# One-core hybrid encoder layer: per-layer embedding transposed first, exponentials split between ACT and DVE, query and key transposes on other PSUM banks, a new slab order

## The chip, the core and the metric

One core of a Trainium2 chip runs the whole layer. The time is the device time of one execution in microseconds (us); three executions of the kernel before gave 777.26, 777.6 and 778.51. Engines: PE (TensorE, matmuls and transposes), ACT (ScalarE), DVE (VectorE), POOL (GpSimd), SP (SyncE, which issues the DMAs).

## The reference, cut to what matters

One layer on 512 tokens of width 1024, all float32:

- h = RMSNorm(x); one projection of h gives attention q (8 heads), k, v (2 heads each) and gate az, delta-rule q, k, v (dq, dk, dv, 8 heads of 128) with decay and beta, gate dz, and two merge gates gA and gB.
- Branch A: q and k are normalised per head, rotated, softmax attention, times SiLU(az), projected (yatt).
- Branch B: short convolution of 5 taps and SiLU on dq, dk, dv, L2 norm, a gated delta rule in chunks, run forward and backward and summed, norm, times SiLU(dz), projected (ydn).
- Merge: sigmoid(gA) * A + sigmoid(gB) * B, projection (out), norm, added to x.
- Per-layer embedding: x + RMSNorm(sigmoid(x W_pg) * (p W_pp)). Here p is 512 x 256; the kernel calls p W_pp "ple" and x W_pg "pg".

## The kernel before, in words

Every large matrix product is done in three passes in a split format: each operand is cut into a high part (ACT casts it to fp32r) and a low part (DVE or POOL subtracts the high part), and PE adds low*high, high*low and high*high. A weight slab is 128 output columns: 512 KB come by DMA into one of two `wraw` buffers, `loader` (L416) and `split` (L211) make `whi` (ACT) and `wlo` (POOL or DVE), two buffers each, and `gemm_t` (L452) runs 24 matmuls of 512 columns into one of five PSUM banks called `mm`. Three further banks are called `aux`.

The order of all instructions is made ahead of time by a small planner, `Flow` (L35). Each part of the work is a generator with a priority (a lower number goes first); the planner keeps a calendar per engine from costs written in the code, and issues the part of the best priority that is ready. The engines then run their instructions in that order, each waiting for its operands on semaphores. `W` reserves DVE and POOL together, `Q` is a DMA issue on SP. Priorities stand in `PR` (L147), and `stream` (L1783) runs, at priority 10, the list `ORDER` (L138): 56 slabs (dk, dq, dv are convolutions; az, dz, gA, gB are gates), the blocks kv, q0, q1, then ydn, yatt, out, pg.

Around the stream, in time:

- Start: `warm_up` (L1708) runs transposes of the identity until planner time WARM. `h_part` (L330) broadcasts the norm's weight over the partitions with two matmuls of one row (L341), `x_norm` (L380) squares x on ACT and scales it on DVE with that broadcast, h is transposed (L357). `ple_part` (L1166) transposes p (L1176) and runs its eight products (L1191 to L1193) at priority 11, below the stream.
- `decay` (L589), and `prep` (L817): the decay factors E of the delta rule, 16 chunks of 128 x 512. A chunk is loaded, masked on POOL, and `exps` (L837) takes eight ACT instructions of 128 x 64, since each half of each head has its own bias `cj`.
- `conv_tail` (L723): per convolution slab, on ACT and DVE, with a transpose.
- The delta rule for head group 0, then 1: `phase_a` (L868), with a substitution of 30 steps on DVE, and `phase_b`; then `phase_y` (L1128).
- `kv_tail` (L1268) and `q_tail` (L1311): norm and rotation of a block that lies in an `mm` bank, then a transpose into another `mm` bank, and the split from there.
- `att_head` (L1367), eight heads, beside the ydn slabs.
- The end: `pg_job` (L1682), whose last tile goes in two halves through `pg_last` (L1650).

Of the kernel before, what the change touches and what calls it, by code (L numbers as in the profile page):

```python
# [16 lines left out]
NT = 4  # L17
# [118 lines left out]


ORDER = """  # L138
dq0 dq3 gB0 dq1 dk1 dq2 dk0 dk2 dk3 dv2 dz4 dk4 dk7 dz3 dv3 dv0
gA5 dz7 dk6 gA3 gB4 az6 dz2 az5 gA2 dv1 dq5 dq4 gA1 dk5 dq6 dq7  # L140
dz0 az2 gA7 dz1 az0 dv7 gB1 dv4 vec az1 az3 dz5 gA0 kv dv5 gB7
dv6 gA4 gB5 az4 gB6 gB3 q0 dz6 gA6 q1 az7 gB2 free_h ydn6 ydn4 ydn7
ydn0 ydn2 ydn5 ydn3 ydn1 yatt0 yatt3 yatt4 yatt1 yatt2 yatt7 yatt6 yatt5 out0 out1 pg0
pg1
"""
OUT0 = 'ydn7 ydn3 ydn3 yatt3'
PR = dict(dec=7, dm1=11, y=4, conv=6, gate=0, kv=9, q=6, head=0, ple=11, prep=4, tab=7)  # L147
GAP = 0.0
X_DVE = ()
WARM = 8.4  # L150
W1 = 0
COOL, HOT = 1.5, -3


@with_exitstack
def layer(ctx, tc, x, p, wt, wba, wn, wpp, npre, rows, qkn, hd16, npost, pnorm, dnorm, cs, out):
# [17 lines left out]
    def G(dur, dep, fn, *a, **k):  # L174
        return op("POOL", dur, dep, fn, *a, **k)

    def Q(kb, dep, o, i):

        t = op("DGE", 0.46, dep, sync.dma_start, o, i)
        return op("DMA", kb * 0.3, t + 0.5, None) + 1.3  # L180

    sb = ctx.enter_context(tc.tile_pool(name="sb", bufs=1))
# [142 lines left out]
        load["dnn"] = Q(0.1, 0.0, dnn, dnorm.rearrange("(p o) -> p o", o=1))  # L325
        first.set(F.now)

    first = Event()

    def h_part():  # L330
        yield "ev", first
        for i in range(4):
            yield "get", f"u{i}"
            (hTh, hTl)[i // 2].append(unit(i, [128, 4, 512], F32R))
        npr, tn = load["npr"]
        yield "at", tn + 0.2
        nb = []
        for half in range(2):
            yield "get", "mm"
            nb.append(bank("mm"))  # L340
            pe.matmul(nb[half], ones[0:1, :], npr[0:1, half * 512:half * 512 + 512], start=True, stop=True)  # L341
        yield "pe", 1.8
        free("blk")
        tn = F.now
        sc = {}
        sc_ev = [Event() for _ in range(NT)]
        spawn(x_norm(sc, sc_ev, nb, tn), 0)
        for t in range(NT):
            xt = load["x", t][0]
            yield "ev", sc_ev[t]  # L350
            for half in range(2):
                yield "at", sc[t, half] + 0.3
                yield "get", "aux"
                pt = bank("aux", [128, 4, 128])
                for j in range(4):
                    k = half * 4 + j
                    pe.transpose(pt[:, j, :], xt[:, k * 128:(k + 1) * 128], ident)  # L357
                yield "pe", 0.45
                cc = slice(t * 128, (t + 1) * 128)
                _, te = split(pt, hTh[half][:, :, cc], hTl[half][:, :, cc], F.now, 512)  # L360
                free("aux", te)
                if t == NT // 2 - 1:
                    h2_ev[half].set(te + 0.2)
                if t == NT - 1:
                    h_ev[half].set(te + 0.2)
        for tag in ("u4", "u5"):
            free(tag)
        rw, t = load["rw"]
        yield "at", t
        yield "get", "aux"  # L370
        pt = bank("aux", [128, 128])
        pe.transpose(pt, rw, ident)
        free("f2", F.now + 0.4)
        yield "pe", 0.11
        t = A(0.2, 0.0, act.copy, cw, pt)
        free("aux", t)
        G(0.1, load["dnn"], pool.tensor_scalar, out=dnn, in0=dnn, scalar1=0.5, scalar2=None, op0=ALU.mult)
        return t
# [434 lines left out]
    LTs, tE = {}, {}  # L813
# [3 lines left out]
    def prep(g, d):  # L817


        away = (g, d) == (1, 1)  # L820
        yield "ev", dec_ev
        if g == 1:
            yield "ev", E_ev[0, 1]
            if d == 0:
                yield "ev", spilled
        u = 16 if away else LTu[g, d]
        yield "get", f"u{u}"
        lt = unit(u, [128, 16, 128])
        sgn = 1 if d == 0 else -1
        for c in range(NT):  # L830
            E = lt[:, 4 * c:4 * c + 4, :]
            t = Q(2, late["CI"], E, CI[d, c, 4 * g:4 * g + 4].unsqueeze(0).to_broadcast([128, 4, 128]))
            yield "at", t - 1.0
            t = G(0.66, t, pool.affine_select, out=E, in_=E, compare_op=ALU.is_ge, fill=-1e30, base=0,
                  pattern=[[0, 4], [sgn, 128]], channel_multiplier=-sgn)

            def exps(E=E, c=c):  # L837
                for h in range(4):
                    for i in range(2):
                        e = E[:, h, i * 64:i * 64 + 64]  # L840
                        act.activation(e, e, AF.Exp, bias=cj[:, d, c, 4 * g + h, i:i + 1])  # L841

            t = A(1.64, t, exps)
            if away:
                t = Q(2, t, E1[c], E)
            tE[g, d, c] = t
        if away:
            free("u16", t)
            spilled.set(F.now)
            yield "get", f"u{LTu[g, d]}"  # L850
            lt = unit(LTu[g, d], [128, 16, 128])
            for c in range(NT):
                tE[g, d, c] = Q(2, tE[g, d, c], lt[:, 4 * c:4 * c + 4, :], E1[c])
        LTs[g, d] = lt
        yield "ev", nj_ev[g]
        for c in range(NT):
            E = lt[:, 4 * c:4 * c + 4, :]

            def scaled(E=E, c=c):
                for h in range(4):  # L860
                    act.activation(E[:, h, :], E[:, h, :], AF.Copy, scale=Nj[:, g, d, c, h:h + 1])

            tE[g, d, c] = either(tE[g, d, c], ("POOL", 1.05, pool.tensor_mul, E, E, bc(Nj[:, g, d, c])), ("ACT", 1.1, scaled))
        E_ev[g, d].set(F.now)

    spilled = Event()

    def phase_a(g):  # L868
        yield "ev", E_ev[g, 0]
# [50 lines left out]
            dve.tensor_sub(w[:, 0:m, m + 1:], w[:, 0:m, m + 1:], tt[:, 0:m, 0:31 - m])  # L920

        chains[0] += 1
        for m in range(30, 0, -1):
            t = W(0.32 + 2 * m * (31 - m) * 0.00104, t - 0.1, step, m)
            yield "at", t - 1.0
# [202 lines left out]
    def phase_y(g, be):  # L1128
# [9 lines left out]
        for c in range(NT):  # L1138
            def scaled(c=c):
                for h in range(4):  # L1140
                    act.activation(o[:, c, h], o[:, c, h], AF.Copy, scale=f[:, c, h:h + 1])

            t = A(1.15, t, scaled)
        us = ((4, 5), (7, 8))[g]
        for u in us:
            yield "get", f"u{u}"
# [16 lines left out]
        y_ev[g].set(t + 0.2)  # L1163


    def ple_part():  # L1166
        yield "ev", first
        yield "get", "u16"
        pT = ple["pT"] = unit(16, [128, 2, 2, 512], F32R)
        pr = ple["p"]  # L1170
        for t_ in range(NT):
            yield "at", ple["tp"] + 0.2
            yield "get", "mm"
            pt = bank("mm", [128, 2, 128])
            for j in range(2):
                pe.transpose(pt[:, j, :], pr[:, t_, j * 128:(j + 1) * 128], ident)  # L1176
            yield "pe", 0.25
            cc = slice(t_ * 128, (t_ + 1) * 128)
            _, t = split(pt, pT[:, 0, :, cc], pT[:, 1, :, cc], F.now, 256)
            free("mm", t)  # L1180
        free("u15")
        yield "at", t + 0.3
        for half in range(2):
            yield "ev", slab["ple", half][0]
            hi, lo = slab["ple", half][1]
# [82 lines left out]
    def kv_tail(t, o, tev):  # L1268
# [15 lines left out]
        free("mm", te)  # L1284
        te = W(0.35, max(te, ts), dve.tensor_mul, kr, kr, sak[:, t, :].unsqueeze(2).to_broadcast([128, 2, 128]))
        yield "at", te + 0.3
        yield "get", "mm"
        pt = bank("mm", [128, 2, 128])
        for h in range(2):
            pe.transpose(pt[:, h, :], kr[:, h, :], ident)  # L1290
        free("f2", F.now + 0.3)
        yield "pe", 0.22
        cc = slice(t * 128, (t + 1) * 128)
        _, te = split(pt, akT[:, 0, :, cc], akT[:, 1, :, cc], F.now, 256)
        free("mm", te)
        return te + 0.2

    att_ev = {}
# [12 lines left out]
    def q_tail(b, t, o):  # L1311
# [8 lines left out]
        te = yield from rope(qs, tabs[0], t, 4, qr, tq)  # L1320
        free("mm", te)
        yield "at", te + 0.3
        yield "get", "mm"
        pt = bank("mm", [128, 4, 128])
        for h in range(4):
            pe.transpose(pt[:, h, :], qr[:, h, :], ident)
        free("f2", F.now + 0.5)
        yield "pe", 0.436
        cc = slice(t * 128, (t + 1) * 128)
        _, te = split(pt, qh[:, :, cc], ql[:, :, cc], F.now, 512)  # L1330
        free("mm", te)
        return max(te, ts) + 0.2


# [315 lines left out]
    def pg_last(t, half, ob, ev):  # L1650
# [25 lines left out]
        for z, at, f in ((late["ob"], 512, V), (ob, 768, V), (z0[:, 0:256], 0, W), (z0[:, 256:512], 256, W)):  # L1676
            x_ = xa[:, at:at + 256]
            tr = f(0.4, tr, dve.scalar_tensor_tensor, out=x_, in0=z, scalar=rs, in1=x_, op0=ALU.mult, op1=ALU.add)
            Q(1, tr, out[t * 128:(t + 1) * 128, at:at + 256], x_)
        return tr  # L1680

    def pg_job(half, us):  # L1682
        if half == 0:
            yield "get", "u4"
            late["z0"] = unit(4, [128, 4, 512])
        for t in range(NT):
            yield "ev", att_ev["x1", t]
            if half == 0 or t < NT - 1:
                o = yield from gemm_n(f"pg{half}", t, sel(x1Th), sel(x1Tl))
                spawn(pg_tail(half, t, o, late["pno_ev"]), 5)  # L1690
        if half == 1:
            t, ev = NT - 1, None
            yield "get", "go"
            e = late["e"] = tile("go", [128, 512])
            late["te"] = Q(2, 0.0, e, eD[t, :, 512:1024])
            yield "get", "c2"
            late["sq"] = tile("c2", [128, 512])
            for i in range(2):
                o = yield from gemm_n("pg1", t, sel(x1Th), sel(x1Tl), cols=slice(i * 256, i * 256 + 256))
                ev = spawn(pg_last(t, i, o, ev), 5)  # L1700
# [31 lines left out]
    spawn(second(), 1)  # L1732
    spawn(phase_y(0, ch0), PR["y"])
    spawn(phase_y(1, y1), PR["y"])
    spawn(ple_part(), PR["ple"])
    for g in range(2):
        for d in ((0, 1), (1, 0))[g]:
# [103 lines left out]
```

## Time and profile before

| what | us |
|---|---|
| median of three runs | 777.6 |
| profiled execution, its own time | 777.5 |
| its span, first to last instruction | 775.7 |
| PE busy | 756.2 |
| DVE busy | 462.5 |
| ACT busy | 360.0 |
| POOL busy | 302.3 |

The span is what the instructions fill; 1.8 us lie around it. An engine counts as busy while an instruction of it is in flight; PE at half clock is busy too, so the granted clock is read beside it.

### The profile page before, as it was taken

The numbers are of one execution on the slowest core, as the hardware profiler recorded it, in microseconds if no ns is written. First come the engines' busy times: TensorE is split into PE (matmuls) and PEld (weight loads), VectorE is DVE, ScalarE is ACT, GpSimd is POOL, SyncE is SP. The second block draws the span as 40 slices with busy tenths as digits, with TensorE's granted clock in tenths as the row PEclk, the third lists the DMA queues.
The fourth block names the chain that finished last, engine by engine and source line by source line (L and its number), as shares of the span: only waits on it lengthen the run. The fifth ranks groups of instructions, "written<-read, shape, count | busy, mean of one in ns | idle before, by whom it ended". The sixth has DMA issues, their size and how long they took to land.

```text
span 775.7 us, 11989 instructions
## 1 busy us (share of the span) xinstructions
PE 756.2 (97%) x4543; PEld 631.2 (81%) x4543; DVE 462.5 (60%) x902; ACT 360.0 (46%) x719; POOL 302.3 (39%) x274
## 2 busy tenths in 40 slices
PE   8998999999999999999999999999999999999995
PEld 6786888888789888888788887778888888888885
DVE  5535767896866677795984543627766734313434
ACT  6477467633552554332542235335556632332422
POOL 4343567302311463102521155557345645561511
PEclk9999999999999999999999999999999999999998
DMA  7272246745310244556220234424233366553213
GB/s 268 96 217 98 81 157 204 200 166 170 104 50 23 78 149 110 187 153 175 86 95 14 68 109 130 127 96 163 82 110 122 110 209 212 198 160 131 95 46 130
DMA packets 53898, 100.50 MB, mean 130 GB/s; under 512 B 21009, under 2 KB 21969, under 8 KB 53842
## 3 DMA queue, kind: packets, MB, share of 16 engines
q1 hardware_dynamic: 53842, 99.75, 39.9%
q8 instruction: 35, 0.57, 0.3%
q14 instruction: 21, 0.17, 0.1%
HBM read 80.83 MB, written 18.91 MB: 129 GB/s over the span
## 4 chain that ended last, share of the span: by engine, by line
PE 80%; ACT 7%; DVE 6%; DMA 2%; issue 2%; POOL 2%; SPq 0%; POOLq 0%; DVEq 0%; ACTq 0%
PE mm L476 14%; PE mm L478 14%; PE mm L477 14%; PE mm L496 4%; PE mm L498 4%; PE mm L497 4%; DVE f L101 3%; ACT u L841 2%; PE mm L515 2%; PE mm L516 2%; PE mm L514 2%; PE aux L1062 2%; PE mm L1415 2%; PE aux L1094 2%; PE aux L1080 1%
## 5 line engine op out<-in xcount | busy, mean ns | idle before, releaser
L101 POOL TENSOR_TENSOR wlo<-wraw,whi 128x1024 fp32r<-128x1024 f32 x68 | 162.6, 2392 | 288.2 <-ACT whi L101 275.8
L476 PE MATMUL mm<-u,wlo 128*128 128x512 f32 x576 | 233.4, 405 | 6.1 <-POOL wlo L101 3.0
L478 PE MATMUL mm<-u,whi 128*128 128x512 f32 x576 | 225.8, 392 | 0.0
L477 PE MATMUL mm<-u,whi 128*128 128x512 f32 x576 | 225.3, 391 | 0.0
L101 ACT CAST whi<-wraw 128x1024 fp32r<-128x1024 f32 x84 | 88.0, 1050 | 126.9 <-PE mm L478 72.0
L476 PEld LDWEIGHTS mm<-u,wlo 128*128 128x128 f32 x576 | 108.7, 189 | 27.1 <-POOL wlo L101 4.2
L478 PEld LDWEIGHTS mm<-u,whi 128*128 128x128 f32 x576 | 108.5, 188 | 23.6
L477 PEld LDWEIGHTS mm<-u,whi 128*128 128x128 f32 x576 | 108.9, 189 | 20.0
L101 DVE SCALAR_TENSOR_TENSOR f<-mm,cw,f 128x510 f32<-128x510 f32 (+1 forms) x96 | 71.9, 749 | 21.2 <-ACT f L101 18.7
L101 DVE TENSOR_TENSOR u<-aux,u 128x512 f32<-128x512 f32 (+1 forms) x56 | 37.7, 689 | 29.3 <-ACT u L101 14.8
L496 PE MATMUL mm<-u,u 128*128 128x512 f32 (+1 forms) x136 | 52.0, 383 | 0.0
L498 PE MATMUL mm<-u,u 128*128 128x512 f32 (+1 forms) x136 | 51.4, 378 | 0.0
L497 PE MATMUL mm<-u,u 128*128 128x512 f32 (+1 forms) x136 | 51.2, 377 | 0.0
L101 POOL TENSOR_TENSOR u<-wraw,u 128x1024 fp32r<-128x1024 f32 x16 | 38.3, 2396 | 19.3 <-ACT u L101 19.2
L514 PE MATMUL mm<-whi,u 128*128 128x512 f32 x96 | 38.0, 396 | 0.0
L515 PE MATMUL mm<-wlo,u 128*128 128x512 f32 x96 | 37.5, 391 | 0.0
L516 PE MATMUL mm<-whi,u 128*128 128x512 f32 x96 | 37.4, 390 | 0.0
L841 ACT ACTIVATE u<-u,cj 128x64 f32<-128x64 f32 x128 | 31.8, 338 | 5.9 <-POOL u L101 5.9
L101 ACT ACTIVATE mm<-f 128x512 f32<-128x512 f32 x24 | 14.4, 600 | 39.3 <-DVE f L101 39.3
L101 ACT COPY c<-aux 128x512 f32<-128x512 f32 x18 | 10.5, 586 | 47.0 <-DVE f L101 27.5
L101 ACT ACTIVATE f<-mm 128x512 f32<-128x512 f32 (+1 forms) x36 | 20.2, 572 | 22.6 <-PE mm L711 8.5
L498 PEld LDWEIGHTS mm<-u,u 128*128 128x128 f32 x136 | 25.6, 188 | 4.9
(245 smaller groups left out, 1272.0 us busy)
## 6 DMA issues: line engine op xcount, KB each, us to landing
wraw<-in_wt_dram SPq DMA_DIRECT2D x72, 512.0 KB, 3.4
wraw<-in_wn_dram SPq DMA_DIRECT2D x28, 512.0 KB, 3.9
u<-CI SPq DMA_DIRECT2D x16, 256.0 KB, 5.3
u<-in_x_dram SPq DMA_DIRECT2D x4, 512.0 KB, 7.3
eD<-c SPq DMA_DIRECT2D x8, 256.0 KB, 2.0
gate_gB<-go SPq DMA_DIRECT2D x8, 256.0 KB, 2.0
gate_dz<-go SPq DMA_DIRECT2D x8, 256.0 KB, 2.1
gate_gA<-go SPq DMA_DIRECT2D x8, 256.0 KB, 2.0
```

The lines of the kernel that those rows point to most:

```text
L101: fn(*a, **k)
L476: pe.matmul(o, lo[:, k, :], mh(k), start=(k == 0), stop=False)
L477: pe.matmul(o, hi[:, k, :], ml(k), start=False, stop=False)
L478: pe.matmul(o, hi[:, k, :], mh(k), start=False, stop=(k == 7))
L496: pe.matmul(o, b, hi, start=(i == 0), stop=False)
L497: pe.matmul(o, a, lo, start=False, stop=False)
L498: pe.matmul(o, a, hi, start=False, stop=(i == 7))
L514: pe.matmul(o[t], b, hi, start=(k == 0), stop=False)
L515: pe.matmul(o[t], a, lo, start=False, stop=False)
L516: pe.matmul(o[t], a, hi, start=False, stop=(k == 7))
L841: act.activation(e, e, AF.Exp, bias=cj[:, d, c, 4 * g + h, i:i + 1])
L1062: pe.matmul(pw[:, h, :], Vm[g][d][:, 4 * c + h, :], r[:, h, :], start=True, stop=True)
```

## The change

The slab order, priorities and a few planner constants change (`COOL`, `HOT` and the new `EXPS` steer choices between engines; costs in the planner are set to 1.94 for the ACT pieces of a chunk, before 1.64, and to 1.25 for scalings, before 1.1 and 1.15). p is transposed by a part of its own of the best priority, in two banks of four transposes each, and the norm's broadcast waits for it (`p_ev`). A chunk's exponentials are either the eight ACT pieces, or one DVE sum and one ACT instruction of 128 x 512, whichever ends first in the planner's calendar. `prep` of group 1, direction 1, waits until group 0's substitution begins. Transposes of q and kv go to `aux` banks. At the end, half of the last tile's output DMAs are issued by ACT, and its embedding is loaded ahead into another buffer.

```diff
 ORDER = """
-dq0 dq3 gB0 dq1 dk1 dq2 dk0 dk2 dk3 dv2 dz4 dk4 dk7 dz3 dv3 dv0
-gA5 dz7 dk6 gA3 gB4 az6 dz2 az5 gA2 dv1 dq5 dq4 gA1 dk5 dq6 dq7
-dz0 az2 gA7 dz1 az0 dv7 gB1 dv4 vec az1 az3 dz5 gA0 kv dv5 gB7
-dv6 gA4 gB5 az4 gB6 gB3 q0 dz6 gA6 q1 az7 gB2 free_h ydn6 ydn4 ydn7
-ydn0 ydn2 ydn5 ydn3 ydn1 yatt0 yatt3 yatt4 yatt1 yatt2 yatt7 yatt6 yatt5 out0 out1 pg0
+dz3 dk2 dq1 dq2 dq3 dk1 dk0 dk3 dq0 dk5 dv3 dk6 dv2 dq7 dq5 dk4
+gB1 dv1 dz0 gA7 gB4 az5 dz7 gB5 gB6 az6 dv0 dz1 dq4 dk7 dz2 gB3
+dz4 dq6 az4 gA0 gA3 dv4 dv5 gA1 dv6 az0 gB0 az2 gA4 gA2 dv7 kv
+vec gA5 gA6 az7 gB2 dz5 q0 dz6 gB7 q1 az3 az1 free_h ydn6 ydn2 ydn7
+ydn4 ydn5 ydn0 ydn3 ydn1 yatt5 yatt3 yatt0 yatt2 yatt1 yatt6 yatt4 yatt7 out0 out1 pg0
 pg1
 """
-PR = dict(dec=7, dm1=11, y=4, conv=6, gate=0, kv=9, q=6, head=0, ple=11, prep=4, tab=7)
+PR = dict(dec=5, dm1=7, y=9, conv=1, gate=0, kv=4, q=5, head=8, ple=5, prep=7, tab=9)
...
-WARM = 8.4
+WARM = 8.2
-COOL, HOT = 1.5, -3
+COOL, HOT = 1.5, -1.5
...
 (h_part)
-        yield "at", tn + 0.2
+        yield "ev", p_ev
+        yield "at", max(F.now, tn) + 0.6
...
             pe.matmul(nb[half], ones[0:1, :], npr[0:1, half * 512:half * 512 + 512], start=True, stop=True)
-        yield "pe", 1.8
+            yield "pe", 0.91
...
 (prep)
         if g == 1:
             yield "ev", E_ev[0, 1]
-            if d == 0:
-                yield "ev", spilled
+            yield "ev", sub_ev if d else spilled
...
-            t = A(1.64, t, exps)
+            def exps2(E=E, c=c):
+                Eh = E.rearrange("p h (s i) -> p h s i", s=2)
+                dve.tensor_add(Eh, Eh, cj[:, d, c, 4 * g:4 * g + 4, :].unsqueeze(3).to_broadcast([128, 4, 2, 64]))
+            ta = F.fit("ACT", 1.94, max(F.now + 0.2, t + 0.15))[0] + 1.94
+            tv = F.slot(("DVE", "POOL"), 0.68, t)[0] + 0.68
+            if ta <= F.fit("ACT", 0.57, tv + 0.15)[0] + 0.57 + EXPS:
+                t = A(1.94, t, exps)
+            else:
+                t = A(0.57, W(0.68, t, exps2), act.activation, E, E, AF.Exp)
...
 (ple_start, spawned at priority -1; the rest of ple_part waits for p_ev)
+        yield "at", ple["tp"] + 0.2
+        for i in range(2):
+            yield "get", "mm"
+            pt = bank("mm", [128, 2, 2, 128])
+            for t_ in range(2):
+                for j in range(2):
+                    pe.transpose(pt[:, j, t_, :], pr[:, 2 * i + t_, j * 128:(j + 1) * 128], ident)
+            yield "pe", 0.5
...
+        p_ev.set(F.now)
...
 (kv_tail and q_tail, the transpose's bank)
-        yield "get", "mm"
-        pt = bank("mm", [128, 4, 128])
+        yield "get", "aux"
+        pt = bank("aux", [128, 4, 128])
...
 (pg_last)
-            Q(1, tr, out[t * 128:(t + 1) * 128, at:at + 256], x_)
+            Q(1, tr, out[t * 128:(t + 1) * 128, at:at + 256], x_, act if at in (512, 0) else sync)
...
 (pg_job, half 1: at its start; before, "go" and "c2" after the third tile)
+            yield "get", "f2"
+            late["e"] = tile("f2", [128, 512])
+            late["te"] = Q(2, 0.0, late["e"], eD[NT - 1, :, 512:1024])
+            yield "get", "f2"
+            late["sq"] = tile("f2", [128, 512])
```

## Rows read from the trace of the kernel before

**Rows 1.** The page, part 1: busy us, share of the span, instructions.
```profile
PE 756.2 (97%) x4543; PEld 631.2 (81%) x4543; DVE 462.5 (60%) x902; ACT 360.0 (46%) x719; POOL 302.3 (39%) x274
```

**Rows 2.** Windows of 20 us: busy per engine, PEclk (granted clock), DMA share, GB/s.
```profile
560.00:580.00 20.00, 20.00 (x105) 16.56 (x105) 12.78 (x31) 11.72 (x25) 9.54 (x9) 1.00 0.37 125
...
760.00:780.00 20.00, 7.93 (x58) 7.37 (x56) 7.21 (x14) 2.75 (x9) 1.89 (x5) 0.84 0.24 86
```

**Rows 3.** Waits of PE: who was waited for, us in total, times, longest.
```profile
PE mm L476 <- POOL wlo L101: 3.0, 1, 3.0
PE mm L476 <- POOL saq L272: 2.4, 2, 1.2
```

**Rows 4.** Timeline, 57 to 67 us: start, us, engine, instruction, [idle before].
```profile
57.59 5.84 ACT L841 ACTIVATE u<-u,cj 128x64 f32<-128x64 f32 x24
...
64.51 2.35 POOL L101 TENSOR_TENSOR wlo<-wraw,whi 128x1024 fp32r<-128x1024 f32 x1 [6.74 <-ACT whi L101]
...
66.91 0.50 PE L476 MATMUL mm<-u,wlo 128*128 128x512 f32 x1 [2.97 <-POOL wlo L101]
```

**Rows 5.** Windows: the 4 us after that wait, and 28 to 108 us.
```profile
68.00:72.00 4.00, 4.00 (x12) 3.12 (x11) 3.60 (x6) 1.39 (x3) 2.32 (x1) 0.57 0.66 228
...
28.00:108.00 80.00, 77.03 (x362) 63.20 (x361) 44.31 (x75) 52.04 (x130) 35.08 (x25) 0.98 0.35 112
```

**Rows 6.** Lines by form: group, count | busy us, mean ns of one | idle before, releaser.
```profile
L841 ACT ACTIVATE u<-u,cj 128x64 f32<-128x64 f32 x128 | 31.8, 338 | 5.9 <-POOL u L101 5.9
...
L101 ACT ACTIVATE mm<-f 128x512 f32<-128x512 f32 x24 | 14.4, 600 | 39.3 <-DVE f L101 39.3
...
L101 DVE TENSOR_TENSOR f<-aux,dj 128x512 f32<-128x512 f32 x12 | 8.3, 691 | 11.9 <-PE aux L1062 11.4 <-ACT c L101 0.5
```

**Rows 7.** Timeline of PE around the transposes of q0 and q1.
```profile
485.59 0.47 PE L476 MATMUL mm<-u,wlo 128*128 128x512 f32 x1 [1.19 <-POOL saq L272]
486.36 0.40 PE L476 MATMUL mm<-u,wlo 128*128 128x512 f32 x1
487.05 0.40 PE L476 MATMUL mm<-u,wlo 128*128 128x512 f32 x1
...
523.33 0.47 PE L476 MATMUL mm<-u,wlo 128*128 128x512 f32 x1 [1.19 <-POOL saq L272]
```

**Rows 8.** The load of p: its issue (us from the start) and its time to landing.
```profile
L101 SPq DMA_DIRECT2D u<-in_p_dram x1: 353/353/353, 1.2 to 1.2; - x1
...
DMA to landing us min/median/max: 3.6/3.6/3.6
```

**Rows 9.** Timeline, 1 to 15 us.
```profile
1.41 1.97 PE L1714 MATMUL mm<-ident 128*128 128x128 f32 x8 [1.41 <-POOL ident masks.py:199]
...
3.31 3.77 PE L341 MATMUL mm<-blk,ones 1*128 1x512 f32 x4
...
7.01 1.11 PE L1176 MATMUL mm<-ident,u 128*128 128x128 f32 x4
...
7.74 0.37 ACT L101 CAST u<-mm 128x256 fp32r<-128x256 f32 x1 [5.67 <-PE mm L1176]
...
10.62 1.07 ACT L101 ACTIVATE blk<-u 128x1024 f32<-128x1024 f32 x1
...
12.73 2.72 DVE L101 SCALAR_TENSOR_TENSOR u<-u,st,mm 128x512 f32<-128x512 f32 x4 [0.23 <-POOL st L264]
```

**Rows 10.** Timeline, 765 to 773 us: the last tile.
```profile
765.09 0.37 ACT L101 ACTIVATE mm<-mm 128x256 f32<-128x256 f32 x1 [2.29 <-PE mm L498]
...
767.97 0.37 ACT L101 ACTIVATE mm<-mm 128x256 f32<-128x256 f32 x1 [1.91 <-PE mm L498]
768.42 0.75 DVE L101 SCALAR_TENSOR_TENSOR mm<-mm,go 128x256 f32<-128x256 f32 x2
...
771.66 0.87 DVE L101 SCALAR_TENSOR_TENSOR wlo<-u,fs,wlo 128x256 f32<-128x256 f32 x2
...
772.28 0.90 SPq L101 DMA_DIRECT2D out_dram<-wlo  x2
```

More of the change, by code (lines that the diff above doesn't have):

```diff
@@ L138 @@
 ORDER = """
-dq0 dq3 gB0 dq1 dk1 dq2 dk0 dk2 dk3 dv2 dz4 dk4 dk7 dz3 dv3 dv0
-gA5 dz7 dk6 gA3 gB4 az6 dz2 az5 gA2 dv1 dq5 dq4 gA1 dk5 dq6 dq7
-dz0 az2 gA7 dz1 az0 dv7 gB1 dv4 vec az1 az3 dz5 gA0 kv dv5 gB7
-dv6 gA4 gB5 az4 gB6 gB3 q0 dz6 gA6 q1 az7 gB2 free_h ydn6 ydn4 ydn7
-ydn0 ydn2 ydn5 ydn3 ydn1 yatt0 yatt3 yatt4 yatt1 yatt2 yatt7 yatt6 yatt5 out0 out1 pg0
-pg1
-"""
-OUT0 = 'ydn7 ydn3 ydn3 yatt3'
-PR = dict(dec=7, dm1=11, y=4, conv=6, gate=0, kv=9, q=6, head=0, ple=11, prep=4, tab=7)
+dz3 dk2 dq1 dq2 dq3 dk1 dk0 dk3 dq0 dk5 dv3 dk6 dv2 dq7 dq5 dk4
[3 more added lines that the diff above has]
+ydn4 ydn5 ydn0 ydn3 ydn1 yatt5 yatt3 yatt0 yatt2 yatt1 yatt6 yatt4 yatt7 out0 out1 pg0
+pg1
+"""
+OUT0 = 'ydn4 ydn5 ydn3 ydn3'
+PR = dict(dec=5, dm1=7, y=9, conv=1, gate=0, kv=4, q=5, head=8, ple=5, prep=7, tab=9)
 GAP = 0.0
+EXPS = 0.0
 X_DVE = ()
-WARM = 8.4
+WARM = 8.2
 W1 = 0
-COOL, HOT = 1.5, -3
+COOL, HOT = 1.5, -1.5
 @with_exitstack
@@ L175, in G, with Q @@
         return op("POOL", dur, dep, fn, *a, **k)
-    def Q(kb, dep, o, i):
-        t = op("DGE", 0.46, dep, sync.dma_start, o, i)
+    def Q(kb, dep, o, i, by=sync):
+        t = op("DGE" if by is sync else "ACT", 0.46, dep, by.dma_start, o, i)
         return op("DMA", kb * 0.3, t + 0.5, None) + 1.3
@@ L326, in first_loads @@
         first.set(F.now)
-    first = Event()
+    first, p_ev = Event(), Event()
     def h_part():
@@ L861, in scaled @@
                     act.activation(E[:, h, :], E[:, h, :], AF.Copy, scale=Nj[:, g, d, c, h:h + 1])
-            tE[g, d, c] = either(tE[g, d, c], ("POOL", 1.05, pool.tensor_mul, E, E, bc(Nj[:, g, d, c])), ("ACT", 1.1, scaled))
+            tE[g, d, c] = either(tE[g, d, c], ("POOL", 1.05, pool.tensor_mul, E, E, bc(Nj[:, g, d, c])), ("ACT", 1.25, scaled))
         E_ev[g, d].set(F.now)
-    spilled = Event()
+    spilled, sub_ev = Event(), Event()
     def phase_a(g):
@@ L922, in phase_a @@
         chains[0] += 1
+        if g == 0:
+            sub_ev.set(F.now)
         for m in range(30, 0, -1):
@@ L1141, in scaled @@
                     act.activation(o[:, c, h], o[:, c, h], AF.Copy, scale=f[:, c, h:h + 1])
-            t = A(1.15, t, scaled)
+            t = A(1.25, t, scaled)
         us = ((4, 5), (7, 8))[g]
@@ L1163, in phase_y, with ple_start @@
         y_ev[g].set(t + 0.2)
-    def ple_part():
+    def ple_start():
         yield "ev", first
@@ L1170, in ple_part @@
         pr = ple["p"]
-        for t_ in range(NT):
-            yield "at", ple["tp"] + 0.2
+        yield "at", ple["tp"] + 0.2
+        for i in range(2):
             yield "get", "mm"
[L1174 to L1179, printed above, removed]
+            pt = bank("mm", [128, 2, 2, 128])
[3 more added lines that the diff above has]
+            yield "pe", 0.5
+            cc = slice(i * 256, (i + 1) * 256)
+            _, t = split(pt.rearrange("p j t c -> p j (t c)"), pT[:, 0, :, cc], pT[:, 1, :, cc], F.now, 512)
             free("mm", t)
+        p_ev.set(F.now)
         free("u15")
-        yield "at", t + 0.3
+        return t
+    def ple_part():
+        yield "ev", p_ev
+        pT = ple["pT"]
+        yield "at", F.now + 1.2
         for half in range(2):
@@ L1286, in kv_tail @@
         yield "at", te + 0.3
-        yield "get", "mm"
-        pt = bank("mm", [128, 2, 128])
+        yield "get", "aux"
+        pt = bank("aux", [128, 2, 128])
         for h in range(2):
@@ L1294, in kv_tail @@
         _, te = split(pt, akT[:, 0, :, cc], akT[:, 1, :, cc], F.now, 256)
-        free("mm", te)
+        free("aux", te)
         return te + 0.2
@@ L1322, in q_tail @@
         yield "at", te + 0.3
-        yield "get", "mm"
-        pt = bank("mm", [128, 4, 128])
+        yield "get", "aux"
+        pt = bank("aux", [128, 4, 128])
         for h in range(4):
@@ L1330, in q_tail @@
         _, te = split(pt, qh[:, :, cc], ql[:, :, cc], F.now, 512)
-        free("mm", te)
+        free("aux", te)
         return max(te, ts) + 0.2
@@ L1685, in pg_job @@
             late["z0"] = unit(4, [128, 4, 512])
+        else:
+            yield "get", "f2"
[3 more added lines that the diff above has]
+            late["sq"] = tile("f2", [128, 512])
         for t in range(NT):
@@ L1692, in pg_job @@
             t, ev = NT - 1, None
[L1693 to L1697, printed above, removed]
             for i in range(2):
@@ L1734, in layer @@
     spawn(phase_y(1, y1), PR["y"])
+    spawn(ple_start(), -1)
     spawn(ple_part(), PR["ple"])
```

## The prediction

> **What bounds the kernel now.** I read the busy shares first. PE is busy 756.2 of 775.7 us, DVE 462.5 and ACT 360.0 [rows 1]: the change takes no product away from PE, so time can come only from the 19.5 us in which PE has nothing in flight, from stretches at half clock, and from the start, where PE runs but waits for h. Windows of 20 us come next: for most of the middle they read as the one of 560 to 580 us does, PE 20.00 of 20.00 [rows 2]. The last window has 7.93 us of PE in the 15.7 us until the end of the span [rows 2], so 7.8 us are a tail behind the last matmul. The list of PE's waits then names two that matter between start and tail: one of 3.0 us for a weight's low part, and twice 1.2 us, 2.4 in all, for something called saq [rows 3].
>
> The first is followed up in the timeline. PE idles 2.97 us until 66.91 for `wlo`; POOL had itself been idle 6.74 us and began the subtraction only at 64.51, when ACT had cast `whi`; and ACT had spent 57.59 to 63.43 on 24 pieces of the exponentials [rows 4]. So ACT sets that wait, through an instruction that is queued behind the exponentials. It has an aftermath: from 68 to 72 us the granted clock is 0.57 on average [rows 5], that is, most of that time at 1.2 instead of 2.4 GHz, after the idle stretch. The loss is (1 - 0.57) x 4 = 1.7 us.
>
> The second sort: after the products of q0 and again of q1, the next slab's first matmul waits 1.19 us [rows 7]. The four results of a q block hold four of the five `mm` banks, the tail's first transpose takes the fifth, and the slab has none. POOL's saq is only what came last in the list of semaphores.
>
> **The change part by part.** The sum is made against the profiled execution's own 777.5 us (span 775.7 and 1.8 around it); the median of the runs is 777.6, so the same sum serves for it.
>
> *Exponentials.* 24 pieces took 5.84 us [rows 4], 0.243 each, 1.95 for a chunk of eight. In the other form a chunk costs ACT one instruction of 128 x 512, 0.60 by the nearest row, and DVE one sum of that size, 0.69 by the nearest [rows 6]. Where DVE and POOL are free that ends after 0.69 + 0.60 = 1.3 us, before the 1.95 of the pieces, so the planner should mostly take it. ACT is spared 1.35 us a chunk; the three chunks just before the late cast spare 4.0, more than the 2.97 of the wait. The wait and the fall of the clock behind it go: 3.0 + 1.7 = 4.7 us. DVE has room: 44.3 of 80 us busy from 28 to 108 us [rows 5], and eight sums of group 0 add 5.5. What is late next there is PE itself. Bounds: nothing gained, if the new plan makes another ACT queue before a cast, to 4.7. The true cost also now stands in the planner (1.94 for 1.64), so what follows a chunk is placed 0.3 us truer. The other eight chunks (the 128 instructions are sixteen chunks [rows 6]) fall where no wait of PE is named: 0.
>
> *A rule that speaks against this.* The sum reads both its inputs from SBUF, and POOL's subtraction of a weight takes 2.35 us [rows 4]; no row shows the two at once. The Trainium skill, SBUF — State Buffer, section "SBUF: two separate sides", says that a DVE operation with two inputs in SBUF and a POOL operation that reads SBUF take one port pair as an exclusive lock, the second being blocked until the first ends. By it three sums could hold POOL back and part of the gain would be lost (the fourth rival has the price).
>
> *q and kv transposes on `aux`.* The fifth `mm` bank is free when the q products end, so the next slab starts at once: two waits of 1.19 us go [rows 7], 2.4 us. Queued behind the transposes on PE are that slab's matmuls, which no longer depend on the tail. `aux` is shared with the delta rule and the heads; q lies between them, kv may meet the delta rule, which then waits for a bank for about a split, ACT 0.6 and DVE 0.7 by rows of that size [rows 6], off PE's path. Bounds: -2.4 to +1.3.
>
> *The start.* p is issued at 1.2 us and lands 3.6 later, at 4.8 [rows 8], but its first transposes ran at 7.01, behind the broadcast of 3.77 us, and ACT began its casts at 7.74; the square of the first x tile came at 10.62 and the scaling at 12.73 [rows 9]. With p first, its eight transposes run from about 4.9 at 0.25 each (8 in 1.97 us [rows 9]) to 6.9; ACT starts at about 6.0, 1.7 us earlier, with the same casts ahead of the square. The broadcast follows at about 7.4 (0.6 us after the transposes) and at the same pace ends at 11.2, before the 12.73 of the scaling less what is won. So the chain of x to h gains between 0 and 1.7 us; ACT is only partly what delays it, and I take 1.2. If the broadcast were late, it would cost at most 11.2 + 1.4 (two scalings) - 12.73, about nothing; bound +1.0. WARM 8.2 drops one warm-up transpose, 0.25 us of work that nothing waits for: 0. The products of p at priority 5 run earlier instead of later; PE's work is the same: 0, and the `c2` buffers and copies they use are off PE's path as long as ACT has room (52.0 of 80 us [rows 5]).
>
> *The end.* The first half's tanh ran at 765.09, but its DVE step was queued with the second half's, both at 768.42 in 0.75 us, after the last tanh at 767.97 [rows 10]. With the embedding there earlier the planner can put the first half's step in front, and the second half is ready 0.4 us earlier. The last DVE step ends at 772.53, the last two issues on SP at 773.18 [rows 10]; on two queues the last begins about 0.2 earlier. Nothing is queued on ACT behind the DMAs it now issues. I take 0.6 us. No row has a DMA issued by ACT: bounds -1.0 (all the lag and as much again) to +0.5 (a longer issue, by one SP issue of 0.45, half of 0.90).
>
> *Order, priorities, `sub_ev`.* No work is added. Convolutions come somewhat earlier, dv and some gates later; the wait for `sub_ev` holds back only exponentials needed by group 1's `phase_a`, long after. A new order has waits of its own. Outside the waits named above, the old one has 19.5 - 7.8 - 3.0 - 2.4 = 6.3 us of idle PE, the start included, and I find no reason why these should all vanish or double. I allow one more wait of the kind seen, 1.2, rounded to 1.4. Bounds -3 (half of the 6.3) to +4.7 (one new wait like the first, with its clock).
>
> **Sum:** 777.5 - 4.7 - 2.4 - 1.2 - 0.6 + 1.4 = 770.0 us.
>
> **The rivals.**
>
> *The ACT queue moves instead of going.* The wait at 66.91 comes back elsewhere, at its full price of 4.7, since each late cast stops PE with only two weight buffers. For it: ACT is the busier of the two helpers from 28 to 108 us, 52.0 against 44.3 [rows 5]. Against it: the sum form needs a third of ACT's time. 777.5 - 2.4 - 1.2 - 0.6 + 1.4 = 774.7.
>
> *The heads lose their filler (slower).* The eight ydn slabs are what PE does while a head waits for its softmax; heads now have priority 8 instead of 0, behind all tails. A slab is 24 matmuls at 0.23 (three in 0.69 [rows 7]), 5.5, the eight 44 us; a head is 24 such matmuls and 16 transposes, about 7.2, the eight 58. If the heads come so late that ydn is done before them, their own chain decides. In the window of 560 to 580 DVE is busy 12.8 and ACT 11.7 of 20 us while PE is full [rows 2]; without filler I estimate a fifth of the heads' 58 us as idle, 12 us. It outweighs the gain once some three quarters of the filler (33 of 44 us, 8.9 lost) have gone. Against it: the stream is at priority 10, still behind the heads. 770.0 - 1.4 + 12 = 780.6.
>
> *It all cancels.* The new order has waits worth what is removed, say two of the first sort without the fall of the clock and one of the second: 777.5 +- 1.5.
>
> *The port lock.* Three sums of 0.69 keep POOL from its subtraction for 2.1 of the 4.0 us won, 1.9 remain against a wait of 2.97, so 1.0 us of it stays, too short to compare with the idle stretch that preceded the fall of the clock: 771.0. That is the Trainium skill's rule, by the page named above; the planner's `W` reserves both engines, which speaks against it.
>
> *All goes well.* The new order also clears half of the remaining idle time: 770.0 - 1.4 - 3 = 765.6.
>
> **How the numbers follow.** Forecast (767.5 to 773) 0.42, with the port lock's 771.0 a further 0.10 in the same range; the moved queue, 774.7, 0.20; all well, 765.6, 0.10; cancelled, 777.5, 0.08; heads, 780.6, 0.10. 0.2% is 1.6 us, about what a measurement of this kernel can tell from no change. Faster by over that (below 776.0) has the first four, 0.82, less 0.02 for the upper edge of the moved queue: 0.80. Same takes that and most of the cancelled case: 0.08. Slower takes the heads and the rest: 0.12. The range for 8 in 10 runs from 765.0, below the case where all goes well, to 778.5, which leaves out the heads and a little below.
>
> **What would show it.** Right: no idle stretch of PE over 1.5 us between 30 and 500 us, and the granted clock at full from the start to the tail; `exps2` sums on DVE, L841's 128 pieces down to a few dozen; no wait of L476 behind the q blocks; the first square of x before 10.6; less than 7.8 us from the last matmul to the end. Wrong: a new wait for `wlo` behind an ACT queue, with a fall of the clock; PE below 19 of 20 us in the windows of the heads; the delta rule's end so late that ydn has to wait for it.

## The result and the profile after

The kernel after took 770.75 us (median of five runs, 769.47 to 773.42) against 777.26 for the kernel before on the same chip, a ratio of 0.992 with an interval of 0.989 to 0.994. Run once more at the end of the study it took 772.69 (six runs, 771.37 to 774.28) against 777.19, ratio 0.995, interval 0.993 to 0.997. So the gain is some 4.5 to 6.5 us; the forecast was 7.5. The profiled execution's own time is 770.75, its span 769.0. One of the five executions of the kernel with the banks alone took 1535.15 us and is left out of that run's numbers.

The page's first part, to be held against [rows 1]:

```profile
PE 753.4 (98%) x4566; PEld 632.5 (82%) x4566; DVE 470.6 (61%) x910; ACT 344.4 (45%) x636; POOL 306.6 (40%) x276
```

PE's idle time is 15.6 us, before 19.5; ACT has lost 15.6 us of work and DVE gained 8. The waits of PE, against [rows 3]:

```profile
PE mm L478 <- POOL wlo L101: 2.0, 2, 1.3
PE mm L1734 <- POOL ident masks.py:199: 1.4, 1, 1.4
PE aux L1309 <- DVE u L101: 1.4, 1, 1.4
PE aux L985 <- issue: 1.1, 2, 0.7
PE mm L1168 <- DVE u L101: 0.8, 1, 0.8
PE mm L713 <- DVE u L101: 0.8, 1, 0.8
```

The two q waits are gone, and the long wait for `wlo` has become two short ones, beside waits for DVE that are new or longer. Windows of the kernel before (two that were not shown) and of the kernel after over the same stretches; columns as in [rows 2]:

```profile
40.00:80.00 40.00, 37.03 (x165) 30.09 (x165) 18.83 (x28) 29.89 (x87) 16.78 (x13) 0.96 0.48 152
480.00:500.00 20.00, 18.28 (x92) 14.62 (x91) 14.84 (x27) 8.36 (x14) 12.79 (x16) 1.00 0.42 131
```
```profile
11.00:14.00 3.00, 3.00 (x8) 2.33 (x8) 1.25 (x2) 2.51 (x5) 0.56 (x1) 0.50 0.75 266
40.00:80.00 40.00, 37.26 (x183) 30.18 (x182) 27.03 (x36) 24.98 (x58) 20.66 (x15) 1.00 0.41 140
480.00:500.00 20.00, 19.18 (x97) 15.61 (x96) 12.61 (x23) 7.95 (x12) 11.54 (x12) 1.00 0.43 136
```

From 40 to 80 us PE is idle 2.74 us instead of 2.97, so hardly less, but the clock is whole: the stretch loses 2.7 us where before it lost 2.97 + 0.04 x 40 = 4.6. The row of 11 to 14 us is new: there the clock is at half.

The start, against [rows 8, 9]:

```profile
1.41 3.68 PE L1734 MATMUL mm<-ident 128*128 128x128 f32 x16 [1.41 <-POOL ident masks.py:199]
...
4.93 1.97 PE L1189 MATMUL mm<-ident,u 128*128 128x128 f32 x8
...
7.47 1.98 PE L343 MATMUL mm<-blk,ones 1*128 1x512 f32 x4
...
8.74 1.06 ACT L101 ACTIVATE blk<-u 128x1024 f32<-128x1024 f32 x1 [0.19 <-DMA u<-in_x_dram]
...
10.85 1.41 DVE L101 SCALAR_TENSOR_TENSOR u<-u,st,mm 128x512 f32<-128x512 f32 x2 [1.40 <-POOL st L265]
...
16.85 4.03 DVE L101 SCALAR_TENSOR_TENSOR u<-u,st,mm 128x512 f32<-128x512 f32 x6
```

And the matmuls of one line of the kernel after, the third pass of p's products (all 16: shortest, median and longest in ns, first and last start):

```profile
L1212 PE MATMUL mm<-u,u x16: 389/394/628, 10.4 to 23.6; 128*128 128x512 f32 x16
```

p's transposes run at 4.93, the first square of x at 8.74 (before 10.62), the scaling at 10.85 (before 12.73): these two come 1.9 us earlier, about the 1.7 that the forecast worked out. But h is not ready earlier; the last row says most of why: all eight products of p now run before 24 us, in front of the transposes of x, and at 628 ns where the clock is at half.

The end, against [rows 10]:

```profile
761.13 0.37 ACT L101 ACTIVATE mm<-mm 128x256 f32<-128x256 f32 x1 [1.53 <-PE mm L500]
761.59 0.42 DVE L101 TENSOR_TENSOR mm<-mm,blk 128x256 f32<-128x256 f32 x1
761.92 0.41 DVE L101 SCALAR_TENSOR_TENSOR mm<-mm,f 128x256 f32<-128x256 f32 x1
...
764.73 0.87 DVE L101 SCALAR_TENSOR_TENSOR wlo<-u,fs,wlo 128x256 f32<-128x256 f32 x2
```

From the last tanh to the last DVE step 4.47 us (761.13 to 765.60), before 4.56; to the end of the span 7.9, before 7.8.

### The profile page after: what moved, and what is told of

It reads as the page before. It is cut to its first block, busy times and chain, and to the rows that moved or that the text cites. A ratio compares the mean times of both kernels' runs of the same rounds, so it can differ in the third digit from the quotient of the medians.

```text
span 769.0 us, 11946 instructions
## 1 busy us (share of the span) xinstructions
PE 753.4 (98%) x4566; PEld 632.5 (82%) x4566; DVE 470.6 (61%) x910; ACT 344.4 (45%) x636; POOL 306.6 (40%) x276
## 4 chain that ended last, share of the span: by engine, by line
PE 90%; DVE 4%; issue 2%; ACT 1%; POOL 1%; DMA 1%; POOLq 0%; DVEq 0%; SPq 0%; ACTq 0%
PE mm L478 15%; PE mm L480 15%; PE mm L479 15%; PE mm L498 4%; PE mm L500 4%; PE mm L499 4%; PE mm L516 3%; PE mm L517 3%; PE mm L518 2%; PE aux L1074 2%; PE mm L1434 2%; PE aux L1106 2%; PE aux L1054 1%; DVE f L101 1%; PE aux L1092 1%
## 5 line engine op out<-in xcount | busy, mean ns | idle before, releaser
L101 POOL TENSOR_TENSOR wlo<-wraw,whi 128x1024 fp32r<-128x1024 f32 x67 | 160.4, 2394 | 300.5 <-ACT whi L101 296.5
L478 PE MATMUL mm<-u,wlo 128*128 128x512 f32 x568 | 229.9, 405 | 2.0 <-POOL wlo L101 2.0
L480 PE MATMUL mm<-u,whi 128*128 128x512 f32 x568 | 222.1, 391 | 0.0
L479 PE MATMUL mm<-u,whi 128*128 128x512 f32 x568 | 221.4, 390 | 0.0
L480 PEld LDWEIGHTS mm<-u,whi 128*128 128x128 f32 x568 | 106.6, 188 | 23.3
L478 PEld LDWEIGHTS mm<-u,wlo 128*128 128x128 f32 x568 | 106.9, 188 | 22.1 <-POOL wlo L101 2.8
L479 PEld LDWEIGHTS mm<-u,whi 128*128 128x128 f32 x568 | 107.0, 188 | 19.3
L101 DVE TENSOR_TENSOR u<-aux,u 128x512 fp32r<-128x512 f32 (+2 forms) x68 | 44.5, 672 | 27.9 <-ACT u L101 20.4
L101 ACT CAST u<-aux 128x512 fp32r<-128x512 f32 (+1 forms) x36 | 20.0, 564 | 35.1 <-PE aux L1607 14.0
L101 ACT ACTIVATE f<-mm 128x512 f32<-128x512 f32 (+1 forms) x38 | 20.9, 562 | 24.5 <-PE mm L713 9.8
```

What stands on the lines that cost most here:

```text
L101: fn(*a, **k)
L478: pe.matmul(o, lo[:, k, :], mh(k), start=(k == 0), stop=False)
L479: pe.matmul(o, hi[:, k, :], ml(k), start=False, stop=False)
L480: pe.matmul(o, hi[:, k, :], mh(k), start=False, stop=(k == 7))
```

## The experiments

All ratios are to the kernel before on the same chip. "Alone" means added to the kernel before, "without" taken from the kernel after.

**The banks alone.**

```diff
-        yield "get", "mm"
-        pt = bank("mm", [128, 4, 128])
+        yield "get", "aux"
+        pt = bank("aux", [128, 4, 128])
```

> The kernel before with one part of the change: the transposes of q and kv go to aux banks. Theory (each part takes away its own wait): the two waits of 1.19 us behind the q blocks go, nothing earlier than kv changes, so 2.4 us faster, about 775.0. Rival (the gain of the change is the redrawn order, the parts are worth little alone): within 1 us of before, the two waits having moved to other instructions of the q tails.

Measured: 772.35 (median of four executions), ratio 0.993 (0.991 to 0.996), 4.7 us faster. The q waits are gone, the wait of 3.0 for `wlo` stays. It is worth more than the two waits: around kv (375 to 380 us) PE is idle 0.86 instead of 1.31 us.

**The exponentials alone** (the diff of `prep` ahead of the prediction).

> The kernel before with one part: a chunk's exponentials by eight ACT pieces or by a DVE sum and one ACT instruction, with the new costs in the planner and the wait for sub_ev. Theory: the wait of 2.97 us at 66.9 and the stretch at 1.2 GHz behind it go, up to 4.7 us faster (772.9), less whatever new wait follows in the same stretch (in the kernel after, 2.7 us of such waits stand between 55 and 72 us). Rival (order): the old order keeps a wait of at least 2.5 us there, 777 or above.

Measured: 776.48, ratio 1.000 (0.998 to 1.002). The stretch from 40 to 80 us loses 1.6 us and the clock holds, so the part does what it says, but other waits stand in the profile now (the first below is the old one of q):

```profile
PE mm L477 <- POOL saq L273: 2.4, 2, 1.2
PE mm L712 <- DVE u L101: 1.6, 1, 1.6
PE aux L984 <- issue: 1.5, 1, 1.5
PE mm L1725 <- POOL ident masks.py:199: 1.4, 1, 1.4
```

The second is a convolution's transpose that waits for DVE until 71.42 us; in DVE's queue ahead of it one sum, begun at 64.11 beside a subtraction on POOL, took 2.82 us instead of 0.68. The profiled execution's span is 1.5 us shorter than before (774.2), which the median does not confirm.

**The start alone** (the diff of `h_part` and `ple_start`).

> The kernel before with one part: p transposed first and the norm's broadcast after it. Theory: 1.2 to 1.7 us faster (about 776.2), with the first square of x at about 8.7 instead of 10.6 us. Rival (the start gains only because the products of p then run at priority 5, filling the wait for h, which this kernel does not have): no change, 777.4, or slower by up to 1.7 us if the clock falls after the broadcast as it does in the profile of the kernel after at 10.9 us.

Measured: 779.48, ratio 1.004 (1.002 to 1.005), 2.5 us slower. Neither theory had the mechanism. The timeline, 58 to 68 us:

```profile
58.25 5.84 ACT L842 ACTIVATE u<-u,cj 128x64 f32<-128x64 f32 x24
...
65.16 2.35 POOL L101 TENSOR_TENSOR wlo<-wraw,whi 128x1024 fp32r<-128x1024 f32 x1 [6.75 <-ACT whi L101]
...
67.56 0.79 PE L477 MATMUL mm<-u,wlo 128*128 128x512 f32 x1 [5.69 <-POOL wlo L101]
```

The ACT queue is the one of [rows 4], piece for piece, but the wait is 5.69 instead of 2.97. In the kernel before, the last products of p filled the rest of it; here is their third pass there, first and last start:

```profile
L1193 PE MATMUL mm<-u,u x16: 388/394/397, 11.8 to 63.6; 128*128 128x512 f32 x16
```

Twelve matmuls, two products, ran there from 61.07 to 63.9 us, some 2.7 us of work, and the wait has grown by 2.72. The new start has run them all by 21 us (they are the same 16), so PE has nothing to do at 61 us. The clock falls to half during the wait, for 6.8 us.

**The order alone** (the lists and constants of the first hunk, with the list of the first output blocks).

> The kernel before with the new slab order, priorities, first output blocks and the constants HOT and WARM, and none of the code changes. Theory (the parts give the gain): about as before, 777, since the queue of exponentials and the q banks still stop PE. Rival (the order gives it): 771 to 773.

Measured: 786.18, ratio 1.012 (1.010 to 1.014), 9.2 us slower, neither number. The order is not worth anything by itself; PE is idle 24.9 us (before 19.5) and busy 3.6 us more, and what the latter comes from stays open:

```profile
PE mm L476 <- POOL wlo L101: 6.1, 4, 3.4
PE mm L476 <- POOL saq L272: 2.4, 2, 1.2
...
PE aux L973 <- issue: 1.2, 2, 0.7
PE aux L1080 <- DVE f L101: 1.1, 1, 1.1
PE aux L1042 <- ACT c L101: 1.0, 2, 0.5
```

**All parts, the old order** (the reverse of that hunk on the kernel after).

> The kernel after with the old slab order, priorities, first output blocks, HOT and WARM: all code changes, none of the order. Theory (the parts give the gain): 770 to 772, the sum of the parts. Rival (the order gives it): 775 or more, with a wait of PE of 2 us or more still in the stretch from 50 to 75 us.

Measured: 774.6, ratio 0.997 (0.996 to 0.999). Neither number: the parts without the order give 2.3 us. The wait in the early stretch is now one for DVE, 3.8 us until 64.31, and the clock falls to half during it. Here too the products of p are over by 21 us; with the exponentials alone two of them run from 61.03 to 63.9, and the transpose behind them waits for nothing:

```profile
PE mm L713 <- DVE u L101: 4.0, 2, 3.8
```

**Without the edits at the end.**

```diff
-            Q(1, tr, out[...], x_, act if at in (512, 0) else sync)
+            Q(1, tr, out[...], x_)
...
+            yield "get", "go"
+            e = late["e"] = tile("go", [128, 512])
```

> The kernel after without its edits at the end (all output DMAs on SP, the last embedding loaded late). The profile of the kernel after shows 7.9 us from the last tanh to the end against 7.8 before, so I expect no difference: 770.7, within 0.5. If the edits are worth the 0.6 us that I forecast and something else took it, this is 0.6 us slower; if the DMAs of ACT cost landing time, 0.3 us faster.

Measured: 770.89, ratio 0.994 (0.992 to 0.996): no difference.

**Without the sum.**

```diff
-EXPS = 0.0
+EXPS = 1e9
```

> The kernel after with every chunk's exponentials as eight ACT pieces (the choice pushed all the way to ACT), costs and waits as after. Theory: ACT is again the queue in front of the weight casts between 45 and 75 us; a wait of PE of 2 us or more and a fall of the clock return, 3 to 5 us slower, about 774.5. Rival (truer costs and the order suffice, the sum is worth nothing, since it also meets POOL): within 1 us of the kernel after.

Measured: 774.65, ratio 0.998 (0.996 to 0.999): 2.0 to 3.9 us slower than the kernel after, by its two medians. The wait came back as forecast, without a fall of the clock:

```profile
PE mm L478 <- POOL wlo L101: 4.5, 2, 3.0
```

**Without the banks** (the reverse of the first diff on the kernel after).

> The kernel after with the transposes of q and kv back in mm banks. Theory (this part takes away its own waits under any order): the two waits of 1.19 us behind the q blocks return, 2.4 to 3.5 us slower than after, about 773.5. Rival (under the new order q and kv have other neighbours and the banks no longer matter): within 1 us of after.

Measured: 775.81, ratio 0.998 (0.997 to 0.999): 3.1 to 5.1 us slower. The first wait below is back, the second is the kernel after's own:

```profile
PE mm L478 <- POOL saq L273: 2.4, 2, 1.2
PE mm L478 <- POOL wlo L101: 2.0, 2, 1.3
```

**Without the start** (the reverse of the diff of `h_part` and `ple_start`).

> The kernel after with the old start: broadcast first, p transposed in four banks at the products' own priority. Theory (the start's gain is that three more products of p run while PE waits for h, in the old order lost again to a longer wait for wlo): h is ready at the same time within 1 us of 24 us, the products end some 9 us later, and the kernel is 1.5 to 4 us slower than after, 772.2 to 774.7. Rival (only the order and the sum matter): within 1 us of after.

Measured: 771.49, ratio 0.993 (0.991 to 0.995). The last product starts at 32.4 us instead of 23.1, as expected, and the last transpose of x at 23.9 instead of 26.8; the time can't be told from the kernel after's, so under the new order the start is worth nothing that these runs show. Its profile has other waits (2.2 for DVE at a convolution's transpose, 2.2 without a releaser in the substitution's join) where the kernel after has the half clock at 11 to 14.

**Two neighbours exchanged.**

```diff
-dz3 dk2 dq1 dq2 dq3 dk1 dk0 dk3 dq0 ...
+dz3 dk2 dq2 dq1 dq3 dk1 dk0 dk3 dq0 ...
```

> The kernel after with two neighbours exchanged in the slab order, dq1 and dq2, the fourth and fifth slabs, which do the same work for two heads of one group. Theory (what counts is the kind of the slabs and the waits that the parts take away): within 0.7 us of after. Rival (the order is fitted to one plan so closely that any redrawing costs): 1.5 us slower or more, with waits of PE at new places.

Measured: 772.86, ratio 0.994 (0.992 to 0.996): 2.1 us above the first measurement of the kernel after, which is the rival's number, but with PE's waits at the old places, not at new ones; beside the second measurement, 772.69, it is no difference.

**A full-height broadcast and another order at the end.**

```diff
-            pe.matmul(nb[half], ones[0:1, :], npr[0:1, half * 512:half * 512 + 512], start=True, stop=True)
+            pe.matmul(nb[half], e0, npr[:, half * 512:half * 512 + 512], start=True, stop=True)
...
+            tz = V(0.38, late["ts0"], dve.tensor_mul, late["ob"], late["ob"], late["pno"][:, 512:768])
             tz = V(0.38, ts, dve.tensor_mul, ob, ob, late["pno"][:, 768:1024])
```

> The kernel after with two additions. The norm's broadcast uses all 128 rows (a matrix with ones in row 0 and zeros below, against a buffer of zeros with the weight in row 0, loaded from ACT's queue); its matmuls are as many and as long. And the first half of the last tile is scaled after the second half's first DVE step instead of before it. Expected: the second half's square 0.3 us earlier after the last tanh, so the end 0.3 us earlier. If the fall of the clock to 1.2 GHz at 10 to 14 us in three profiles of this start comes from the one-row matmuls before it, no fall shows and the products of p take 1.4 us each there, up to 1.7 us won: 769.0 to 770.4 in all. If it does not come from them, the fall stays and only the 0.3 us are won. The slower side: POOL's clearing of the buffer delays the broadcast, under 1 us.

Measured: 773.21, ratio 0.994 (0.993 to 0.996): not better. The broadcast came late for a reason that I had not listed, the weight's own load:

```profile
4.10 0.52 ACTq L101 DMA_DIRECT2D blk<-in_npre_dram  x1
...
9.07 3.46 PE L346 MATMUL mm<-blk,e 128*128 128x512 f32 x4 [2.29 <-DMA blk<-in_npre_dram]
```

Issued by ACT at 4.10, in the middle of the loads of x, 4 KB took until 9.07. The clock fell at 9.4 us, but behind an idle stretch of 2.3, so whether one-row matmuls have a part in it stays open; in the start alone and under the old order the same four one-row matmuls ran without a fall behind them. The end did what it should: from the last tanh to the last DVE step 4.14 us (764.39 to 768.53) instead of 4.47.

**The kernel after again.**

> The kernel after, unchanged, once more. Without the tail edits (770.89), without the new start (771.49) and with two neighbours exchanged (772.86) it came within 2.1 us of the 770.75 that were measured for it. If start and exchange are worth what these medians say, this kernel comes out at 769.5 to 771.2 again, with waits of PE where its first profile had them. Rival: the same program spreads by that much, because the clock falls or does not fall after the start, and its waits in the short matmuls of the substitution's join differ from execution to execution: 771.5 to 773, and then the start, the tail and the exchange are worth nothing that can be told.

Measured: 772.69. The rival holds. Over the eleven runs of this program the time goes with the mean granted clock: 769.47 at 0.997, 770.75 at 0.995, 772.25 at 0.994, 773.42 at 0.993, 774.28 at 0.992. Its profile has the kernel after's waits at the same places, with other lengths (2.5 for `wlo`, 1.7 without a releaser).

## Why the prediction was right

The time lies in the range and on the forecast's side, and two of the terms were right in mechanism. Not all of it was right for its reasons: too much was expected of the exponentials (by 2.8 us), the start (1.2) and the end (0.5), too little of the banks (0.7 to 2.7) and of the order, which was charged as a loss. That these errors cancel, so that the sum of 770.0 lies 0.75 us from the first median, is luck. Two of the signs named for it did not come: the clock fell at 10.9 us, and 7.9 us lie behind the last matmul, not less than 7.8. The heads kept their filler: from 540 to 760 us PE is busy 20.00 of every 20 us.

- **Exponentials, 4.7 us.** Mechanism right, size wrong: the wait of 2.97 and the 1.7 of half clock went, but the stretch has new waits of 2.7 us, so 1.9 us net there by the profiles. Leaving the sum out costs 2.0 to 3.9 us; alone the part gains 0.5, which can't be told from nothing. I had charged new waits to the order, 1.4 us, and not to this part, which makes DVE the next to be late: 27.0 busy of 40 us against 18.8.
- **The port lock** was a rival at 0.10, and the lock is there. Timeline of the kernel after:

```profile
59.24 2.40 POOL L101 TENSOR_TENSOR wlo<-wraw,whi 128x1024 fp32r<-128x1024 f32 x1
...
59.46 2.74 DVE L846 TENSOR_TENSOR u<-u,cj 128x512 f32<-128x512 f32 x1
...
62.23 0.63 ACT L101 ACTIVATE u<-u 128x512 f32<-128x512 f32 x1 [1.47 <-DVE u L846]
...
66.68 0.66 PE L713 MATMUL mm<-ident,u 128*128 128x128 f32 x4 [0.76 <-DVE u L101]
...
67.80 1.03 ACT L101 CAST whi<-wraw 128x1024 fp32r<-128x1024 f32 x1
...
68.96 4.75 POOL L101 TENSOR_TENSOR wlo<-wraw,whi 128x1024 fp32r<-128x1024 f32 x2 [6.27 <-ACT whi L101]
...
71.41 0.50 PE L478 MATMUL mm<-u,wlo 128*128 128x512 f32 x1 [1.31 <-POOL wlo L101]
```

One of the ten sums takes 2.74 us where the median is 0.684; it ends 0.56 us after POOL's subtraction has ended at 61.64. That agrees with the Trainium skill, SBUF — State Buffer, section "SBUF: two separate sides": a DVE operation with both inputs in SBUF is blocked while POOL reads there. It was DVE that lost, and once: POOL's subtraction took its usual 2.40 (the select that follows it on POOL took 1.09 us, where four in a row took 2.40). The planner reserves both engines, but the chip's times had moved apart from the plan's. The same kind of sum (2.73 to 2.82 us) shows in five further kernels. As priced, with POOL held back for 2.1 us, the rival did not come; through DVE a loss of its size may have. DVE, held for 2.06 us, then works with hardly a gap until 67.23; the convolution's transpose waits 0.76 us for it, and ACT's cast of 67.80 stands behind exponentials that wait for its sums, so that `wlo` is late by 1.31 us at 71.41. These two waits are 2.07 of the stretch's 2.74 us. No run takes the meeting with POOL away, so what it costs is read from this chain and not shown.
- **q and kv on `aux`, 2.4 us.** Right, and too small: 4.7 alone, 3.1 to 5.1 when taken away. Of kv I said that its wait might cost the delta rule; its waits shrank instead. This is the largest part, and the only one that is shown to work under either order.
- **The start, 1.2 us.** The step failed. The casts came 1.7 us earlier, as worked out, and the first square and scaling 1.9, but the last transpose of x started at 26.8 instead of 23.9 us. DVE scaled the second tile at 16.85, where it had been about 14.1: copies of p's products, one of which waited 2.19 us for PE, and a weight's split stood ahead of it, and POOL's step for the scale had stood behind a cast that ACT made at 12.96. The prediction had those copies "off PE's path as long as ACT has room". The last scaling ended at 20.9 (before 19.7), and PE came to the transposes only behind the products of p, at 23.8, with the clock at half from 10.9 to 14.3. I had put those products at nothing, "PE's work is the same". They are work done while h is awaited, three products of 1.36 us, and two of them were also the cover of the wait at 61 us. Under the old order that cover is missed, without the sum (a wait of 5.69 us) and with it (3.8); under the new order taking the start away changes nothing that can be told.
- **The end, 0.6 us.** Failed: 0.1 in the DVE chain, none in the time. The planner did place the first half's step earlier, but its scaling, which waited for nothing, then stood in front of the second half's step (761.59 and 761.92). The last experiment moved it and won the 0.3 in that chain.
- **The order, +1.4 us.** Wrong in kind. Alone it costs 9.2 us, with the parts it gains 1.9 to 3.9. It is no sum of waits with a price of its own but fits one set of parts.
- **The sum.** The four parts add up, alone, to -4.7 - 0.5 + 2.5 and nothing for the end (not run alone), -2.7; all together under the old order they gave -2.3. So the parts nearly add, and the rest of the gain is the order made for them.

## What to carry to other kernels

Where PE is busy 97% of the time, read its few waits and ask of each what ran inside it: work that fills one wait is missed when it is moved away. A hand-made order is worth something only with the parts for which it was made, so try a new order and the new parts together, and take each part away from the result as well as adding it to the start. Measure the same program twice before reading a difference of 2 us out of 770.

## What the runs showed of the hardware

- A DVE sum with both inputs in SBUF, 0.68 us, took 2.74 beside POOL's subtraction.
- The 4 KB load issued by ACT among loads of 512 KB took 5 us to be of use; outputs of 128 KB issued by ACT at the end landed in a median of 1.9 us, those issued by SP in 2.1, but in the kernel before, with all four on SP, in 1.8.
- In bursts of 128 matmuls of 32 x 32 (L985) PE stops for 0.2 to 1.9 us with no releaser in the profile, at the same places but with other lengths in each execution. The cause stays open.
- Four matmuls of one row took 3.77 us in the kernel before and 1.98 after, where they came behind transposes alone. The windows give a granted clock of 1.00 there in both, but the trace's first clock record begins at 10.3 us before and at 7.45 after; that the clock was at half until then is read from the pace, eight transposes in 1.97 us and later in 1.03. In six profiles of this start under the new order it fell again at 9.4 to 10.9 us for 3.4 us; in the start alone the record begins at 4.7, and the clock stayed up until the wait at 61.
